# Preparing the seven-product pairs in three pieces and starting a head's attention every five ticks

## The chip, the cores and the metric

The kernel runs on one core of one Trainium2 chip. A core has five engines that work side by side, each through its own instructions in program order: TensorE (PE; its weight loads are shown as PEld), VectorE (DVE), ScalarE (ACT), GpSimd (POOL) and SyncE (SP), which here only starts transfers. The metric is the device time of one execution in microseconds (us); the median of several runs is given.

## The reference

One layer of a decoder: MoBA attention with 16 heads of 128, then a SwiGLU feed-forward block, each followed by a residual and a layer normalisation. There are 256 tokens of width 2048 and the inner width is 5632. With 256 tokens there is one MoBA block, so attention is plain causal attention with a bias by distance (T5 buckets).

```python
q, k, v = jnp.split(x @ w_qkv, 3, axis=-1)          # 256 x 2048 each, 16 heads
...
l_own = (jnp.einsum('bhqd,bhjd->bhqj', qc, k_own).astype(jnp.float32)
         + bias_h[:, t5_bucket(qpos[:, None] - kpos_own[None, :])].astype(jnp.float32))
p = masked_softmax(...)                              # causal
return ... + jnp.einsum('bhqj,bhjd->bhqd', p[..., n_sel:], v_own)
...
x = layer_norm(ALPHA * x + h, ln1_g[i], ln1_b[i])    # h = attention @ w_o
x = layer_norm(ALPHA * x + swiglu(x, ffn_w_gate[i], ffn_w_up[i], ffn_w_down[i]), ln2_g[i], ln2_b[i])
```

## The kernel before

**Sections, blocks and ticks.** Every large product is a *section*: `q0` to `q5` (the twelve 512-column chunks of `w_qkv`, two a section), `o0`, `o1` (`w_o`), `f0` to `f10` (a chunk of `w_gate` and one of `w_up` each) and `d` (`w_down`). A section goes through eight (`d`: 22) *pairs* of 128-row slices of its weights. The program is one list of *blocks*, PE's matmuls for one pair and one half of the rows or products; the index in that list is the *tick*. Ticks 18 to 33 are q1, 34 to 49 q2, 50 to 65 q3, 66 to 81 q4, 82 to 97 q5, 98 to 113 o0.

**Split numbers.** Each fp32 operand is taken as a high and a low part in `fp32r`: ACT copies it to the high part (L86), DVE subtracts (L87), and a product of two such operands is three matmuls (L278 to L280, or L342, L343 and L346).

**Seven products.** Sections q1 to q5 and f1 to f10 combine the halves of the rows so that fewer products are needed. In most pairs a half block is 12 matmuls. Pairs 1, 3 and 5 (`ST`) use a scheme with seven products: the first half block is 9 matmuls and the second 12. Such a pair is prepared by `split_quad`: two loads, four sums on DVE (`t13`, `t24`, L257 to L260), and the splits of `gq`, `uq` (raw) and of `aq`, `bq` (from the sums). A section of this kind keeps seven sums (`acc`) in seven of the eight PSUM banks; `sums_1`, `sums_2`, `sums_3` read them out four ticks before its last, one before and behind it. Banks are taken from the front of one queue (`bank`) and put back at its end (`give`), so a step that takes a bank waits until its last reader is done with it.

**Order.** At each tick the program writes first the work registered with `before`, then the pieces (load and split of a pair) whose start is due, then the block, then the work registered with `after`. A pair's pieces start 3 ticks ahead of its first block in the q sections (`AHEAD`), 6 or 5 in the f sections (`ST_AHEAD`), other numbers in places (`LEAD`, `EARLY`). Every engine executes its part of this order strictly. Tiles come from pools: `p4` (38 of 4 KB), `s2` (12 of 2 KB), `raw` (6, the loaded weights).

**Attention.** A group of four heads needs q, k from one section and v from another. A head goes through five steps: `at_t1` (four transposes of q and k into one bank, split into `qkh`, `qkl`), `at_s` (scores in a bank, bias and maximum on DVE, exponentials on ACT), `at_n` (reciprocal on DVE, scaling on ACT; no bank), `at_t2` (three transposes of the probabilities, split; split of v) and `at_o` (product with v, copied to the group's tile `o`). `att_steps` orders a group's steps, two heads at a time, so that a pair of heads takes eight ticks:

```python
one = [[(at_t1, a)], [(at_t1, b)], [(at_s, a)], [(at_s, b), (at_n, a)],
       [(at_n, b), (at_t2, a)], [(at_t2, b)], [(at_o, a)], [(at_o, b)]]
```

Group 0 runs in q2, group 1 in q3, group 2 in q5, group 3 in o0 (with fewer ticks); q4 has no attention. The results of groups 0 to 2 go to DRAM (`od`) and come back (`load_o`) before o0 needs them (`split_o`). `gate_t` transposes the hidden values of an f section through one bank each.

Of the kernel before, what the change touches and what calls it, by code (L numbers as in the profile page):

```python
# [11 lines left out]
F = mybir.dt.float32  # L12
# [4 lines left out]
P = 128  # L17
S = 256
# [19 lines left out]
AHEAD = 3  # L38
AHEAD_Q = 5
# [1 line left out]
SQK, SV = {0: 0, 1: 2, 2: 3, 3: 5}, {1: (0, 1), 4: (2, 3)}  # L41
KEEP = 2
ST = (1, 3, 5)
ST_AHEAD = {True: 6, False: 5}
WARM = 9
LEAD = {("f1", 0): 4, ("f1", 1): 3, ("d", 0): 6, ("d", 1): 4}
EARLY = {0: -1, 1: 0, 2: 1, 3: 2}


# [1 line left out]
def decoder_layer(ctx: ExitStack, tc: tile.TileContext, x, xt, rel_bias, w_qkv, w_o, g1, b1, gb1,  # L51
# [6 lines left out]
    dr = ctx.enter_context(tc.tile_pool(name="dr", bufs=1, space=bass.MemoryType.DRAM))  # L58
    ctx.enter_context(tc.manual_schedule())

    def p4(shape, dt, name):
        return sb.tile(shape, dt, tag="p4", bufs=P4, name=name)

    def s2(shape, dt, name):
        return sb.tile(shape, dt, tag="s2", bufs=S2, name=name)
# [6 lines left out]
    def bank(name):  # L72
        n = free.popleft()
        t = ps.tile([P, CW], F, tag=f"b{n}", bufs=1, name=name)
        held[id(t)] = (t, n)
        return t

    def give(*ts):
        for t in ts:
            free.append(held.pop(id(t))[1])  # L80

    def f32(t):
        return t.bitcast(F)

    def split(hi, lo, src):
        nc.scalar.activation(hi, src, AF.Copy)  # L86
        nc.vector.tensor_tensor(lo, src, f32(hi), op=OP.subtract)  # L87
# [11 lines left out]
    def load_x(p, ks):  # L99
        if p not in x_raw:  # L100
            x_raw[p] = s2([P, 2, S], F, f"xr{p}")
        nc.sync.dma_start(x_raw[p][:, ks, :], xt[p][:, ks, :])

    def split_x(p, ks):
        hi, lo = xT[p // 2]
        a = 2 * (p % 2)
        split(hi[:, a + ks.start:a + ks.stop, :], lo[:, a + ks.start:a + ks.stop, :], x_raw[p][:, ks, :])
# [15 lines left out]
    gbT = const.tile([P, 32], F, name="gbT")  # L123

    rows = dr.tile([H, RL], F, name="rows")
    od = dr.tile([3, P, 4 * S], F, name="od")
    bias_t = {}

    def load_small():
# [41 lines left out]
    def h_lhs(kt, m):  # L171
# [4 lines left out]
    Q = [Sec(f"q{n}", [(w_qkv, 4 * i + g) for i, g in pair], 8, x_lhs, xC if n else None)  # L176
         for n, pair in enumerate(QKV)]
    WO = [Sec(f"o{i}", [(w_o, 2 * i + c) for c in range(2)], 8, o_lhs) for i in range(2)]
    NF = FF // CW
    FU = [Sec(f"f{i}", [(w_gate, i), (w_up, i)], 8, x1_lhs, x1C if i else None) for i in range(NF)]  # L180
    DN = Sec("d", [(w_down, c) for c in range(4)], FF // (2 * P), h_lhs)
# [3 lines left out]
    def add(sec, pairs, m, chunks=None, ks=(0, 1)):  # L185
        blocks.append((sec, pairs, m, range(len(sec.chunks)) if chunks is None else chunks, ks))
        return len(blocks) - 1
# [13 lines left out]
    k = 8 - SKEW_WO  # L201
    alternate(WO[1], 0, k)
    wo_t = [[add(WO[1], list(range(k, 8)), m, [c]) for c in range(2)] for m in range(2)]
# [4 lines left out]
    k = DN.npair - SKEW_D  # L208
# [7 lines left out]
    first, last = {}, {}  # L216
# [4 lines left out]
    start = {k: t - AHEAD for k, t in first.items()}  # L221
    for p in range(1, 8):
        start["q0", p] = first["q0", p] - AHEAD_Q
    for p, t in EARLY.items():
        start["f0", p] = wo_t[0][0] + t
    for s in [*Q[1:], *FU[1:]]:
        for p in range(s.npair):
            start[s.name, p] = first[s.name, p] - (AHEAD if s in Q else ST_AHEAD[p in ST])
    for (n, p), a in LEAD.items():
        start[n, p] = first[n, p] - a  # L230
    order = sorted(((start[s.name, p], first[s.name, p], s, p) for s in [*Q, *WO, *FU, DN] for p in range(s.npair) if s is not Q[0] or p),
                   key=lambda v: (v[1], v[3]))

    def load_piece(s, p, c):
        w, col = s.chunks[c]
        r = sb.tile([P, 2, CW], F, tag="raw", bufs=RAW, name=f"r_{s.name}_{p}_{c}")
        src = w[p, col]
        if s is not Q[0] or p:
            nc.sync.dma_start(r, src)
        s.raws[p, c] = r, src  # L240

    def split_piece(s, p, c):
        if (p, c) not in s.raws:
            load_piece(s, p, c)
        r, _ = s.raws.pop((p, c))
        hi = p4([P, 2, CW], R, f"wh_{s.name}_{p}_{c}")
        lo = p4([P, 2, CW], R, f"wl_{s.name}_{p}_{c}")
        split(hi, lo, r)
        s.pieces[p, c] = (hi, lo)

    def split_quad(s, p):
        for c in range(2):
            if (p, c) not in s.raws:
                load_piece(s, p, c)
        (g, _), (u, _) = (s.raws.pop((p, c)) for c in range(2))
        t13, t24 = p4([P, 2, CW], F, "t13"), p4([P, 2, CW], F, "t24")
        nc.vector.tensor_tensor(t13[:, 0, :], g[:, 0, :], u[:, 0, :], op=OP.add)  # L257
        nc.vector.tensor_tensor(t13[:, 1, :], u[:, 0, :], u[:, 1, :], op=OP.add)  # L258
        nc.vector.tensor_tensor(t24[:, 0, :], t13[:, 0, :], u[:, 1, :], op=OP.add)
        nc.vector.tensor_tensor(t24[:, 1, :], t24[:, 0, :], g[:, 1, :], op=OP.add)  # L260
        g2 = [p4([P, 2, CW], R, "gq") for _ in range(2)]
        u2 = [s2([P, CW], R, "uq") for _ in range(2)]
        a2 = [p4([P, 2, CW], R, "aq") for _ in range(2)]
        b2 = [p4([P, 2, CW], R, "bq") for _ in range(2)]
        split(*g2, g)
        split(*u2, u[:, 1, :])
        split(*a2, t13)
        split(*b2, t24)
        at = lambda t, k: tuple(v[:, k, :] for v in t)
        s.pieces[p, 0] = s.pieces[p, 1] = {1: at(g2, 0), 2: at(g2, 1), 3: u2, 5: at(a2, 0), 7: at(a2, 1),  # L270
                                           6: at(b2, 0), 4: at(b2, 1)}

    def product(s, n, lhs, rhs, stop):
        start = n not in s.acc
# [107 lines left out]
    sums = {}  # L382
# [72 lines left out]
    def at_o(h):  # L455
        g, j = divmod(h, 4)
        hi, lo, vh, vl = att.pop(h)
        if j == 0:
            oT[g] = (p4([P, 4, S], R, f"oh{g}"), p4([P, 4, S], R, f"ol{g}")) if g == 3 else p4([P, 4, S], F, f"o{g}")
        b = bank("ov")  # L460
        n = 0
        for m, o, ks, w in ((0, 0, 0, 2 * P), (1, P, 2 * P, P)):
            for a, c in ((vh, hi), (vh, lo), (vl, hi)):
                nc.tensor.matmul(b[:, o:o + w], a[:, m, :], c[:, ks:ks + w], start=n == 0, stop=n == 5)
                n += 1
        if g == 3:
            oh, ol = oT[g]
            split(oh[:, j, :], ol[:, j, :], b[:, :S])
        else:
            nc.scalar.activation(oT[g][:, j, :], b[:, :S], AF.Copy)  # L470
            if j == 3:
                nc.scalar.dma_start(od[g], oT.pop(g))
        give(b)

# [9 lines left out]
    def att_steps(g):  # L484
        steps = []
        for a in (4 * g, 4 * g + 2):
            b = a + 1
            one = [[(at_t1, a)], [(at_t1, b)], [(at_s, a)], [(at_s, b), (at_n, a)],
                   [(at_n, b), (at_t2, a)], [(at_t2, b)], [(at_o, a)], [(at_o, b)]]
            if g == 3:  # L490
                one = [one[0] + one[1], one[2], one[3], one[4][:1], one[4][1:], one[5], one[6] + one[7]]
            steps += one
        return steps
# [156 lines left out]
    def before(t, f, *a):  # L650
        pre.setdefault(t, []).append((f, a))

    def after(t, f, *a):
        post.setdefault(t, []).append((f, a))
# [16 lines left out]
    for g in range(4):  # L671
        if g:
            at_sums(Q[SQK[g]], qk_sums, g)
        t0 = (first["q2", 0], first["q3", 0], first["q5", 0], first["o0", 0])[g]
        before(t0 - 3, load_bias, g)
        for n, step in enumerate(att_steps(g)):
            for f, h in step:
                after(t0 + n, f, h)
        if g < 3:
            after(first["o0", 2 * g] - 5, load_o, g)  # L680
            after(first["o0", 2 * g] - 3, split_o, g)
    after(last["o0", 0] - 6, reload_x)
    for m in range(2):
        for c in range(2):
# [19 lines left out]
    t = dn_t[0][0] - 32  # L704
# [5 lines left out]
    for i in range(NF):  # L710
        t = last[f"f{i}", 1]
# [10 lines left out]
    for i in range(NF):  # L722
        t = first["d", 2 * i]
# [14 lines left out]
    s = Q[0]  # L738
# [13 lines left out]
    n = 0  # L752
    for t, blk in enumerate(blocks):
        for f, a in pre.get(t, []):
            f(*a)
        while n < len(order) and order[n][0] <= t:
            _, _, ss, p = order[n]
            if ss is Q[0]:
                load_x(p, slice(0, 2))
                split_x(p, slice(0, 2))  # L760
            if ss.comb is not None and p in ST:
                split_quad(ss, p)
            else:
                for c in range(len(ss.chunks)):
                    split_piece(ss, p, c)
            n += 1
        block(*blk)
        for f, a in post.get(t, []):
            f(*a)
# [49 lines left out]
```

## Time and profile before

| what | value |
|---|---|
| median of 3 runs | 1145.39 us (1144.97 to 1145.89) |
| the profiled execution's own time | 1146.3 us |
| its span, first to last instruction | 1144.5 us |
| mean granted TensorE clock | 0.988 |
| busy: PE, PEld, DVE, ACT, POOL | 1105.3, 908.7, 867.8, 591.5, 10.3 us |
| read from HBM, written | 224.55 MB, 10.51 MB |

The profile is of one execution. Busy times of different engines overlap. PE's matmuls are pipelined and their ends are modelled, so that a busy PE is not PE at its peak. [...]

### The profile page before, as it was taken

Reading aid. Unit: us, or ns where it says so; the run is one execution under the profiler, and the core shown is the slowest. Engines: PE = TensorE matmul, PEld = TensorE weight load, DVE = VectorE, ACT = ScalarE, POOL = GpSimd, SP = SyncE. Lnnn points to the kernel's source line nnn. Section 1 sums busy time; section 2 is a strip of 40 time slices with the busy share of each in tenths; the row PEclk is TensorE's granted clock in tenths of the full one; section 3 lists DMA queues with packets and bytes.
Section 4 is the critical chain, followed back from the end, with each engine's and each line's share of the span. In section 5 each row is a group of like instructions: output and inputs, shape, how many; then the busy total and the mean of one; then the engine's idle time right before and its main releaser. Section 6 shows DMA issues by size and latency. Waiting matters only on the chain.

```text
span 1144.5 us, 13666 instructions
## 1 busy us (share of the span) xinstructions
PE 1105.3 (97%) x5004; PEld 908.7 (79%) x5004; DVE 867.8 (76%) x1124; ACT 591.5 (52%) x782; POOL 10.3 (1%) x16
## 2 busy tenths in 40 slices
PE   9998988998999999999999999999999999999995
PEld 6887777786778887788888888888888888888884
DVE  6897677788676867988988988988989546574446
ACT  6564555555556635655646646646647435353320
POOL 0000000000000000000000000000000000000001
PEclk9999998999999999999999999999999999999998
DMA  9574444473584825667566556556549595486611
GB/s 339 196 253 156 153 141 133 157 262 130 183 281 161 312 93 183 236 212 253 174 212 240 183 204 239 194 192 239 202 170 338 183 340 220 167 329 245 233 37 74
DMA packets 66611, 235.96 MB, mean 206 GB/s; under 512 B 7600, under 2 KB 8048, under 8 KB 66544
## 3 DMA queue, kind: packets, MB, share of 16 engines
q1 hardware_dynamic: 63632, 224.58, 56.2%
q10 hardware_dynamic: 2304, 8.39, 1.8%
q0 software_dynamic: 608, 2.12, 0.5%
q8 instruction: 39, 0.64, 0.2%
q14 instruction: 28, 0.23, 0.1%
HBM read 224.55 MB, written 10.51 MB: 205 GB/s over the span
## 4 chain that ended last, share of the span: by engine, by line
PE 82%; DVE 10%; ACT 4%; issue 2%; DMA 1%; SPq 0%; POOL 0%; ACTq 0%; DVEq 0%; POOLq 0%
PE acc_f L278 12%; PE acc_f L280 12%; PE acc_f L279 12%; PE acc_d L342 7%; PE acc_d L343 7%; PE acc_d L346 7%; PE acc_q L278 4%; PE acc_q L280 4%; PE acc_q L279 4%; PE acc_o L342 2%; PE acc_o L343 2%; PE acc_o L346 2%; PE acc_q L343 1%; PE acc_q L346 1%; PE acc_q L342 1%
## 5 line engine op out<-in xcount | busy, mean ns | idle before, releaser
L87 DVE TENSOR_TENSOR wl_d<-r_d,wh_d 128x1024 fp32r<-128x1024 f32 x88 | 104.4, 1222 | 71.5 <-ACT wh_d L86 50.8
L87 DVE TENSOR_TENSOR wl_f<-r_f,wh_f 128x1024 fp32r<-128x1024 f32 x116 | 135.2, 1219 | 16.1 <-ACT wh_f L86 15.9
L342 PE MATMUL acc_d<-wh_d,hh 128*128 128x512 f32 x352 | 137.0, 389 | 0.0
L343 PE MATMUL acc_d<-wl_d,hh 128*128 128x512 f32 x352 | 136.9, 389 | 0.0
L86 ACT ACTIVATE wh_d<-r_d 128x1024 fp32r<-128x1024 f32 x88 | 90.5, 1057 | 75.0 <-DMA r_d<-in_w_down 46.1
L86 ACT ACTIVATE wh_f<-r_f 128x1024 fp32r<-128x1024 f32 x116 | 115.7, 1049 | 9.1 <-DMA r_f<-in_w_up 4.0
L278 PE MATMUL acc_f<-wh_f,x1h 128*128 128x512 f32 x300 | 116.9, 390 | 0.0
L280 PE MATMUL acc_f<-wh_f,x1l 128*128 128x512 f32 x300 | 116.7, 389 | 0.0
L279 PE MATMUL acc_f<-wl_f,x1h 128*128 128x512 f32 x300 | 116.7, 389 | 0.0
L86 ACT ACTIVATE aq<-t 128x1024 fp32r<-128x1024 f32 x45 | 47.7, 1060 | 124.5 <-DVE t L258 114.6
L346 PE MATMUL acc_d<-wh_d,hl 128*128 128x512 f32 x352 | 99.9, 389 | 0.0
L87 DVE TENSOR_TENSOR wl_q<-r_q,wh_q 128x1024 fp32r<-128x1024 f32 x64 | 75.6, 1221 | 12.4 <-ACT wh_q L86 11.9
L346 PEld LDWEIGHTS acc_d<-wh_d,hl 128*128 128x128 f32 x352 | 66.1, 188 | 13.7
L342 PEld LDWEIGHTS acc_d<-wh_d,hh 128*128 128x128 f32 x352 | 66.1, 188 | 13.7
L343 PEld LDWEIGHTS acc_d<-wl_d,hh 128*128 128x128 f32 x352 | 66.1, 188 | 13.6
L86 ACT ACTIVATE wh_q<-r_q 128x1024 fp32r<-128x1024 f32 x64 | 64.1, 1048 | 3.3 <-DMA r_q<-in_w_qkv 2.9
L280 PEld LDWEIGHTS acc_f<-wh_f,x1l 128*128 128x128 f32 x300 | 56.3, 188 | 11.8
L278 PEld LDWEIGHTS acc_f<-wh_f,x1h 128*128 128x128 f32 x300 | 56.3, 188 | 11.6
L279 PEld LDWEIGHTS acc_f<-wl_f,x1h 128*128 128x128 f32 x300 | 56.3, 188 | 11.6
L278 PE MATMUL acc_q<-wh_q,xh 128*128 128x512 f32 x150 | 62.7, 418 | 0.0
L280 PE MATMUL acc_q<-wh_q,xl 128*128 128x512 f32 x150 | 60.2, 401 | 0.0
L279 PE MATMUL acc_q<-wl_q,xh 128*128 128x512 f32 x150 | 59.9, 399 | 0.0
(268 smaller groups left out, 2409.7 us busy)
## 6 DMA issues: line engine op xcount, KB each, us to landing
r_q<-in_w_qkv SPq DMA_DIRECT2D x94, 512.0 KB, 4.3
r_f<-in_w_gate SPq DMA_DIRECT2D x88, 512.0 KB, 3.8
r_f<-in_w_up SPq DMA_DIRECT2D x88, 512.0 KB, 4.9
r_d<-in_w_down SPq DMA_DIRECT2D x88, 512.0 KB, 6.1
r_o<-in_w_o SPq DMA_DIRECT2D x32, 512.0 KB, 4.4
hd<-hT ACTq DMA_DIRECT2D x9, 512.0 KB, 6.2
hT<-hd SPq DMA_DIRECT2D x9, 512.0 KB, 3.5
bias<-rows POOLq DMA_DIRECT2D x4, 512.0 KB, 5.6
```

Of the source, the lines that this page charges most:

```text
L86: nc.scalar.activation(hi, src, AF.Copy)
L87: nc.vector.tensor_tensor(lo, src, f32(hi), op=OP.subtract)
L278: nc.tensor.matmul(a, lh, rh, start=start, stop=False)
L279: nc.tensor.matmul(a, lh, rl, start=False, stop=False)
L280: nc.tensor.matmul(a, ll, rh, start=False, stop=stop)
L342: nc.tensor.matmul(a, lh, hi[:, k, :], start=kt == 0, stop=False)
L343: nc.tensor.matmul(a, lh, lo[:, k, :], start=False, stop=False)
L346: nc.tensor.matmul(s.acc[m, c], ll, hi[:, k, :], start=False, stop=kt == nk - 1)
```

## The change

`split_quad` becomes three functions, `quad_sums`, `quad_raw` and `quad_low`, that stand at three ticks one after another: in q sections 4, 3 and 2 ticks ahead of the pair's first block, in f sections 6, 5 and 4 (4, 3 and 2 for pair 1 of f1). The other pairs keep their starts. The list of pieces is sorted by start, not by first block. Attention of groups 0 to 2 no longer follows `att_steps`: a head's five steps stand three ticks apart, the heads five ticks apart, the groups twenty, from tick 34 on, so that heads of two groups follow each other through q4, and the last step of the twelfth head falls on tick 101. Group 3 keeps its place and steps. Group 2's result stays on the chip. `load_bias` stands two ticks ahead of a group, not three.

```diff
-ST_AHEAD = {True: 6, False: 5}
-LEAD = {("f1", 0): 4, ("f1", 1): 3, ("d", 0): 6, ("d", 1): 4}
+LEAD = {("d", 0): 6, ("d", 1): 4}
...
-    od = dr.tile([3, P, 4 * S], F, name="od")
+    od = dr.tile([2, P, 4 * S], F, name="od")
...
-    order = sorted(((start[s.name, p], first[s.name, p], s, p) for s in [*Q, *WO, *FU, DN] for p in range(s.npair) if s is not Q[0] or p),
-                   key=lambda v: (v[1], v[3]))
+    order = []
+    for s in [*Q, *WO, *FU, DN]:
+        for p in range(s.npair):
...
+            f = first[s.name, p]
+            if s.comb is None:
+                todo = [(start[s.name, p], "plain")]
+            elif p in ST:
+                a = 4 if s in Q or (s is FU[1] and p == 1) else 6
+                todo = [(f - a, "sums"), (f - a + 1, "raw"), (f - a + 2, "low")]
+            else:
+                todo = [(f - (3 if s in Q else 4 if s is FU[1] and not p else 5), "plain")]
+            order += [(t, f, p, what, s) for t, what in todo]
+    order.sort(key=lambda v: v[:3])
...
-    def split_quad(s, p):
+    quad = {}
+
+    def quad_sums(s, p):
         for c in range(2):
-            if (p, c) not in s.raws:
-                load_piece(s, p, c)
+            load_piece(s, p, c)
         (g, _), (u, _) = (s.raws.pop((p, c)) for c in range(2))
         t13, t24 = p4([P, 2, CW], F, "t13"), p4([P, 2, CW], F, "t24")
...
+        quad[s.name, p] = g, u, t13, t24
+
+    def quad_raw(s, p):
+        g, u, t13, t24 = quad[s.name, p]
         g2 = [p4([P, 2, CW], R, "gq") for _ in range(2)]
         u2 = [s2([P, CW], R, "uq") for _ in range(2)]
+        split(*g2, g)
+        split(*u2, u[:, 1, :])
+        s.pieces[p, 0] = {1: at_k(g2, 0), 2: at_k(g2, 1), 3: u2}
+
+    def quad_low(s, p):
+        _, _, t13, t24 = quad.pop((s.name, p))
         a2 = [p4([P, 2, CW], R, "aq") for _ in range(2)]
         b2 = [p4([P, 2, CW], R, "bq") for _ in range(2)]
-        split(*g2, g)
-        split(*u2, u[:, 1, :])
         split(*a2, t13)
         split(*b2, t24)
...
-            if j == 3:
+            if j == 3 and g < 2:
                 nc.scalar.dma_start(od[g], oT.pop(g))
...
-        t0 = (first["q2", 0], first["q3", 0], first["q5", 0], first["o0", 0])[g]
-        before(t0 - 3, load_bias, g)
-        for n, step in enumerate(att_steps(g)):
-            for f, h in step:
-                after(t0 + n, f, h)
-        if g < 3:
+        t0 = first["q2", 0] + 20 * g if g < 3 else first["o0", 0]
+        before(t0 - 2, load_bias, g)
+        if g == 3:
+            for n, step in enumerate(att_steps(g)):
+                for f, h in step:
+                    after(t0 + n, f, h)
+            continue
+        for j in range(4):
+            for f, n in ((at_t1, 0), (at_s, 3), (at_n, 6), (at_t2, 9), (at_o, 12)):
+                after(t0 + 5 * j + n, f, 4 * g + j)
+        if g < 2:
             after(first["o0", 2 * g] - 5, load_o, g)
-            after(first["o0", 2 * g] - 3, split_o, g)
+        after(max(first["o0", 2 * g] - 3, t0 + 28), split_o, g)
```

## Rows read from the trace of the kernel before

**Rows 1.** The page: engines' busy time; the chain that ended last, by engine.
```profile
PE 1105.3 (97%) x5004; PEld 908.7 (79%) x5004; DVE 867.8 (76%) x1124; ACT 591.5 (52%) x782; POOL 10.3 (1%) x16
...
PE 82%; DVE 10%; ACT 4%; issue 2%; DMA 1%; SPq 0%; POOL 0%; ACTq 0%; DVEq 0%; POOLq 0%
```

**Rows 2.** Stretches: their us, engines' busy us (instructions), granted clock, DMA share, GB/s.
```profile
94.20:318.40 224.20, 203.39 (x962) 167.53 (x962) 172.45 (x284) 123.08 (x212) 2.25 (x3) 0.95 0.50 166
...
480.00:1130.00 650.00, 650.00 (x2907) 538.13 (x2907) 493.82 (x550) 322.67 (x357) 0.99 (x1) 1.00 0.61 216
```

**Rows 3.** What PE waited for, whole span: us in total, times, longest.
```profile
PE t L447 <- ACT sc L441: 16.9, 6, 4.3
PE t L406 <- DVE k L379: 4.7, 2, 3.9
PE ht L631 <- ACT hT L632: 2.5, 1, 2.5
```

**Rows 4.** Timeline ahead of two waits of `at_t2`: start, us, engine, line, operation.
```profile
104.88 0.69 DVE L257 TENSOR_TENSOR t<-r_q,r_q 128x512 f32<-128x512 f32 x1
...
110.29 1.22 DVE L87 TENSOR_TENSOR bq<-t,bq 128x1024 fp32r<-128x1024 f32 x1
111.42 0.42 DVE L423 CUSTOM_DVE_ANT_0 sc<-lg,bias 128x256 f32<-128x256 f32 x1
...
113.19 0.49 ACT L440 ACTIVATE sc<-sc,rs 128x256 f32<-128x256 f32 x1
...
114.03 0.90 PE L447 MATMUL t<-ident,sc 128*128 128x128 f32 x3 [4.29 <-ACT sc L441]
...
143.20 0.55 PE L447 MATMUL t<-ident,sc 128*128 128x128 f32 x3 [1.50 <-ACT sc L441]
```

**Rows 5.** Timeline at tick 50, the transposes of k.
```profile
160.66 0.69 PE L406 MATMUL t<-ident,k 128*128 128x128 f32 x2 [3.92 <-DVE k L379]
```

**Rows 6.** Stretches about the long waits and one between them, columns as in rows 2.
```profile
112.50:119.30 6.80, 5.27 (x14) 4.30 (x15) 3.62 (x7) 4.85 (x12) 0.00 (x0) 0.50 0.06 17
160.30:163.70 3.40, 3.04 (x8) 2.47 (x9) 1.74 (x3) 2.32 (x3) 0.00 (x0) 0.50 0.50 205
177.30:184.10 6.80, 5.75 (x15) 4.57 (x16) 3.59 (x6) 4.48 (x10) 0.00 (x0) 0.50 0.15 33
279.80:283.10 3.30, 3.30 (x11) 2.62 (x10) 1.94 (x3) 3.04 (x6) 0.00 (x0) 0.50 0.00 0
119.40:160.20 40.80, 35.83 (x183) 29.53 (x181) 30.04 (x51) 21.26 (x39) 0.76 (x1) 1.00 0.48 159
```

**Rows 7.** Timeline at f0 to f1, the two `gate_t`.
```profile
477.77 0.58 ACT L632 ACTIVATE hT<-ht 128x512 f32<-128x512 f32 x1
...
478.40 0.66 PE L631 MATMUL ht<-ident,hn 128*128 128x128 f32 x4 [2.51 <-ACT hT L632]
```

**Rows 8.** Stretches without attention: of q4's length, and of f sections, columns as before.
```profile
215.00:256.50 41.50, 41.50 (x187) 34.44 (x186) 35.94 (x43) 23.21 (x27) 0.75 (x1) 1.00 0.75 253
...
530.00:800.00 270.00, 270.00 (x1215) 223.52 (x1214) 232.41 (x272) 146.97 (x170) 0.00 (x0) 1.00 0.62 213
```

**Rows 9.** Timeline of ACT and DVE behind `at_s`, `at_t2`, and `at_n`.
```profile
200.91 0.51 ACT L431 ACTIVATE sc<-sc,nm 128x256 f32<-128x256 f32 x1 [2.99 <-DVE nm L429]
...
202.88 2.36 DVE L87 TENSOR_TENSOR wl_q<-r_q,wh_q 128x1024 fp32r<-128x1024 f32 x2 [2.01 <-ACT wh_q L86]
...
212.53 2.36 DVE L87 TENSOR_TENSOR wl_q<-r_q,wh_q 128x1024 fp32r<-128x1024 f32 x2 [0.37 <-ACT wh_q L86]
...
331.77 0.49 ACT L440 ACTIVATE sc<-sc,rs 128x256 f32<-128x256 f32 x1
...
333.54 2.36 DVE L87 TENSOR_TENSOR wl_o<-r_o,wh_o 128x1024 fp32r<-128x1024 f32 x2 [2.43 <-ACT wh_o L86]
```

**Rows 10.** What DVE and ACT waited for from 94 to 322 us.
```profile
DVE qkl L87 <- ACT qkh L86: 8.1, 5, 1.9
...
ACT gq L86 <- DMA r_q<-in_w_qkv: 0.8, 1, 0.8
```

More of the change, by code (lines that the diff above doesn't have):

```diff
@@ L225, in decoder_layer @@
         start["f0", p] = wo_t[0][0] + t
-    for s in [*Q[1:], *FU[1:]]:
-        for p in range(s.npair):
-            start[s.name, p] = first[s.name, p] - (AHEAD if s in Q else ST_AHEAD[p in ST])
+    for p in range(1, 8):
+        start["q0", p] = first["q0", p] - AHEAD_Q
     for (n, p), a in LEAD.items():
         start[n, p] = first[n, p] - a
-    order = sorted(((start[s.name, p], first[s.name, p], s, p) for s in [*Q, *WO, *FU, DN] for p in range(s.npair) if s is not Q[0] or p),
-                   key=lambda v: (v[1], v[3]))
+    for p, t in EARLY.items():
+        start["f0", p] = wo_t[0][0] + t
+    order = []
+    for s in [*Q, *WO, *FU, DN]:
+        for p in range(s.npair):
+            if s is Q[0] and not p:
+                continue
[9 more added lines that the diff above has]
+    order.sort(key=lambda v: v[:3])
     def load_piece(s, p, c):
@@ L260, in split_quad, with at_k, plain @@
         nc.vector.tensor_tensor(t24[:, 1, :], t24[:, 0, :], g[:, 1, :], op=OP.add)
+        quad[s.name, p] = g, u, t13, t24
+    def at_k(t, k):
+        return tuple(v[:, k, :] for v in t)
+    def quad_raw(s, p):
+        g, u, t13, t24 = quad[s.name, p]
         g2 = [p4([P, 2, CW], R, "gq") for _ in range(2)]
         u2 = [s2([P, CW], R, "uq") for _ in range(2)]
+        split(*g2, g)
[3 more added lines that the diff above has]
+        _, _, t13, t24 = quad.pop((s.name, p))
         a2 = [p4([P, 2, CW], R, "aq") for _ in range(2)]
         b2 = [p4([P, 2, CW], R, "bq") for _ in range(2)]
-        split(*g2, g)
-        split(*u2, u[:, 1, :])
         split(*a2, t13)
         split(*b2, t24)
-        at = lambda t, k: tuple(v[:, k, :] for v in t)
-        s.pieces[p, 0] = s.pieces[p, 1] = {1: at(g2, 0), 2: at(g2, 1), 3: u2, 5: at(a2, 0), 7: at(a2, 1),
-                                           6: at(b2, 0), 4: at(b2, 1)}
+        s.pieces[p, 0].update({5: at_k(a2, 0), 7: at_k(a2, 1), 6: at_k(b2, 0), 4: at_k(b2, 1)})
+    def plain(s, p):
+        if s is Q[0]:
+            load_x(p, slice(0, 2))
+            split_x(p, slice(0, 2))
+        for c in range(len(s.chunks)):
+            split_piece(s, p, c)
     def product(s, n, lhs, rhs, stop):
@@ L673, in decoder_layer @@
             at_sums(Q[SQK[g]], qk_sums, g)
-        t0 = (first["q2", 0], first["q3", 0], first["q5", 0], first["o0", 0])[g]
-        before(t0 - 3, load_bias, g)
-        for n, step in enumerate(att_steps(g)):
-            for f, h in step:
-                after(t0 + n, f, h)
-        if g < 3:
+        t0 = first["q2", 0] + 20 * g if g < 3 else first["o0", 0]
[4 more added lines that the diff above has]
+                    after(t0 + n, f, h)
+            continue
+        for j in range(4):
+            for f, n in ((at_t1, 0), (at_s, 3), (at_n, 6), (at_t2, 9), (at_o, 12)):
+                after(t0 + 5 * j + n, f, 4 * g + j)
+        if g < 2:
             after(first["o0", 2 * g] - 5, load_o, g)
-            after(first["o0", 2 * g] - 3, split_o, g)
+        after(max(first["o0", 2 * g] - 3, t0 + 28), split_o, g)
     after(last["o0", 0] - 6, reload_x)
@@ L756, in decoder_layer @@
         while n < len(order) and order[n][0] <= t:
[L757 to L765, printed above, removed]
+            _, _, p, what, ss = order[n]
+            {"plain": plain, "sums": quad_sums, "raw": quad_raw, "low": quad_low}[what](ss, p)
             n += 1
```

## The prediction

> **What bounds the kernel now.** I read the page's engine table first, then the chain that ended last, then TensorE's busy time in stretches, then what TensorE waited for, and then the timeline around the longest waits. The table shows PE busy for 1105.3 us of 1144.5, and the chain runs 82% through PE and 10% through DVE [rows 1]. So PE sets the time, and only its idle stretches and its clock can be won back. The stretches say where those lie. From 480 to 1130 us PE has no idle microsecond [rows 2]; the feed-forward part has nothing to give. The 224.2 us from 94.2 to 318.4 are ticks 34 to 97, sections q2 to q5, where attention is interleaved with the products: PE is idle there for 20.8 us and its mean granted clock is 0.95 [rows 2].
>
> The list of PE's waits names three [rows 3]. The transposes of the probabilities (`at_t2`, L447) wait six times, 16.9 us in all, for ScalarE's normalisation (`at_n`). The transposes of q and k (`at_t1`, L406) wait twice, 4.7 us, for the last sum of k. The transpose of the first hidden block (`gate_t`, L631) waits once, 2.5 us. No wait of PE is for a DMA.
>
> The timeline shows what is late ahead of the first of the six [rows 4]. A quad's eight DVE instructions run in one piece from 104.88 to 111.42 us. The scores of head 1 lie ready in their bank, but their reduction stands behind the quad and begins at 111.42; the exponentials and the normalisation follow, and PE, which wants the probabilities of head 0 one tick after `at_n`, goes on only at 114.03 after 4.29 us. In tick 50 it is the same queue: the last sum of k runs behind a quad and lets PE go at 160.66 after 3.92 us [rows 5]. [...] The wait of 1.50 us at 143.20 lies in a stretch at 1.00 [rows 4, 6].
>
> **The change, part by part.** *Three pieces instead of one.* No instruction is added or removed: the two loads and four sums go to tick f-4 of a Q section, two splits to f-3, two to f-2 (f is the pair's first product), where all stood at f-3. Per tick DVE then has about 2.5 us of sums, 1.7 us (a split of 1.13 and one of half its size, 0.6) or 2.3 us (two of 1.13), not 6.5 us at once [rows 4]. Nothing comes too late by itself: the low pieces are for the second half block, at f+1. The loads' SP queue is governed by the six `raw` tiles, which the raw splits still release at f-3; ACT waited 0.8 us for weights in this stretch [rows 10]. I cost it at nothing; were that cover gone, a load would show up as an ACT wait. In the f sections the splits end one and two ticks later than before, but PE never waits there (270 us, no idle) and DVE is busy 232.4 of 270 us [rows 8]; nothing again.
>
> *Attention at five-tick steps.* A head now takes t1, s, n, t2, o at distances of three ticks, and a head starts every five ticks from tick 34 to 89. With n and t2 three ticks (some 8 us) apart, the six waits of L447 lose their cause: 16.9 us. Group 1 starts at tick 54, five ticks behind its sums, so the 3.92 us at tick 50 go; the other wait for k, 0.8 us, I leave, because group 3 keeps its place. With these the 8.7 us of clock go. The work itself stays: PE without these losses needs 224.2 - 20.8 - 8.7 = 194.7 us for the 64 ticks. Only the last two steps of head 11 move to ticks 98 and 101, behind which group 3's first transposes queue on PE; they wait for k there anyway.
>
> *f0 to f1.* The 2.5 us are a bank: the second `gate_t` needs the bank of the first, whose copy ran at 477.77, queued on ACT behind the two late splits of a quad [rows 7]. In the new order those splits (the "low" of pair 3) come two ticks after that copy's place, and pair 1's begin two ticks earlier. I take the 2.5 us as gone.
>
> *Group 2's store and reload* fall away, `load_bias` goes one tick nearer to its group on POOL's queue, but still five ticks ahead of `at_s`. Nobody waited for these: nothing.
>
> Losses removed: 16.9 + 3.9 + 2.5 + 8.7 = 32.0 us.
>
> **What comes in their place.** DVE was hidden half the time by PE's waiting. A section without attention costs DVE 35.94 us in the 41.5 us that PE needs [rows 8]. The stretch has 172.45 us of DVE work [rows 2], so a head costs DVE (172.45 - 4 x 35.94)/12 = 2.4 us; PE pays (194.7 - 4 x 41.5)/12 = 2.4 us for one too. In five ticks, one head, that is 13.6 us of DVE against 15.2 of PE: it fits. But DVE and ACT run in program order, and a split's low part waits for ACT's high part, which stands behind the step of the tick before. After the scores' reduction ACT does two exponentials and then the high split, and DVE stands for 2.0 us. After `at_n` ACT does the two scalings and the split: from 331.77 to 333.54, 1.8 us. After t2 it is 0.37 us [rows 9]. The loss arises only if the next tick begins with a split, not with sums or nothing. I went through the ticks: of 12 score steps 8 are followed by a split (ticks 38, 43, 53, 58, 63, 73, 83, 93), of 12 `at_n` also 8 (41, 51, 61, 66, 71, 81, 86, 91), of 12 t2 also 8. So DVE needs 172.5 + 8 x 2.0 + 8 x 1.8 + 8 x 0.37 = 205.9 us for 64 ticks of which PE could do in 194.7: PE must wait 11 us in total.
>
> It feels that through the banks: from a section's fourth to its twelfth tick seven of eight hold sums, so each step needs the bank of the step before it, read by DVE. Walking ticks 34 to 97 in order with these prices (a block of 12 matmuls 2.7 us by 187 in 41.5 us [rows 8], one of 9 2.0) gives waits of 3, 4, 5 and 5 us in q2 to q5, mostly 0.5 to 2.4 us each, where t2 needs the bank of the scores and t1 that of t2. The walk charged DVE 36.9 us a section, about 1 us too many in each, so 17 becomes 13, near the sum's 11. I take 13. Its ends: 0, if DVE's lag is absorbed everywhere; and, if every head pays 2.0 and the 2.43 us that one `at_n` shows with an exponential ahead of it, 0.37 and also the longest wait of `qkl`, 1.9 us [rows 9, 10], 13.6 + 6.7 = 20.3 against 15.2 us, 61 us for 12 heads.
>
> The profiled execution took 1146.3 us, 1.8 more than its span and 0.9 more than the median. 1146.3 - 32.0 + 13 = 1127.3; against the median 1126.4. I write 1126.5.
>
> **The rivals.** *PE-bound throughout.* DVE's waits fall into its own slack; everything is won: 1146.3 - 32.0 - 0.9 = 1113.4, up to 1119 with less than 6 us of new waits. For it speaks that DVE is busy only 172 of 194.7 us; against it the 2 us waits, which the order of the queues fixes.
>
> *Many short waits hold the clock down.* By the rows above only idle stretches of 3.7 us and more came with 0.50. If the new waits, close together, also draw it, with two drops a section at the mean price of before (8.7/4 = 2.2 us), 17 us more: 1144. One drop a section: 1135. [...]
>
> *DVE becomes the bound: slower.* One mechanism, the DVE-ACT-DVE turn after each step, in ticks 34 to 97. It decides when a head costs DVE and its turns 32/12 = 2.7 us more than PE's 15.2 us for five ticks; I count 13.6 + 2.0 + 1.8 + 0.4 = 17.8 when none of them is absorbed, 2.6 more, right at break-even; at the upper end, 20.3, it is 1146.3 - 32 + 61 - 0.9 = 1174. For it: quiet q4 loses its slack too, where DVE stood free today. Against it: a third of the turns is followed by sums or by nothing.
>
> *It does nothing:* the waits move from n-t2 to the banks in the same size, 28 to 36 us of new waits: about 1145.
>
> **How the numbers follow.** Chances: partial gain, 6 to 22 us of new waits, 0.57 (1119 to 1136, likeliest 1126.5); PE-bound 0.20 (1113 to 1119); clock 0.13 (1136 to 1144); nothing 0.04; slower 0.06. Whether a run differs can be told from about 0.2% on, 2.3 us. Faster by more: 0.57 + 0.20 + 0.13 = 0.90; within: 0.04; slower: 0.06. For 8 in 10 the range reaches from 1114 to 1140: half of the clock's cases, nothing and slower stay outside, together some 0.17.
>
> **What would show it.** In the changed profile: no L447 wait for `at_n`'s scaling; L406, L447 or L464 waiting 0.5 to 2.5 us for DVE's `ptl`, `qkl` or the scores' reduction, from the fourth tick of a section on; DVE busy about 83% of 208 us between the first product of q2 and of o0, against 77% of 224.2; granted clock 1.00 there; no 2.5 us ahead of L631. I am wrong if that stretch takes under 200 or over 218 us, if 0.50 still appears in it, if quads' pieces make PE wait (matmuls of `acc_q` waiting for a split), or if the f sections show idle time.

## The result and the profile after

The changed kernel takes 1128.82 us in the median (1128.10 to 1129.13, 4 runs), the kernel before 1145.64 (1144.97 to 1147.88, 4 runs): a ratio of 0.9849, 95% interval 0.9832 to 0.9866. The forecast was 1126.5 us, with a range from 1114 to 1140. The profiled execution took 1129.13 us, its span is 1127.0.

The engine table and the chain by engine, for [rows 1]:

```profile
PE 1099.1 (98%) x5004; PEld 904.6 (80%) x5004; DVE 866.9 (77%) x1124; ACT 589.3 (52%) x782; POOL 10.3 (1%) x16
...
PE 80%; DVE 11%; ACT 4%; issue 2%; DMA 1%; SPq 0%; POOL 0%; ACTq 0%; DVEq 0%; POOLq 0%
```

The instructions on the engines are the same in number; what PE lost to idle time and to a lower clock changed. Stretches of the changed kernel: ticks 34 to 97, the two places in them with a lower clock, and the f sections, with the columns of [rows 2, 6, 8]:

```profile
93.40:303.80 210.40, 198.07 (x952) 162.42 (x951) 168.75 (x279) 119.24 (x208) 2.25 (x3) 0.98 0.53 178
127.80:131.30 3.50, 3.50 (x11) 2.78 (x10) 2.25 (x3) 2.49 (x3) 0.00 (x0) 0.51 0.56 213
264.40:267.80 3.40, 3.40 (x10) 2.63 (x9) 3.37 (x6) 0.15 (x1) 0.00 (x0) 0.50 0.65 217
530.00:800.00 270.00, 270.00 (x1219) 223.48 (x1218) 234.30 (x277) 148.67 (x174) 0.00 (x0) 1.00 0.59 207
```

The 64 ticks take 210.4 us where they took 224.2. PE is idle for 210.4 - 198.07 = 12.3 us instead of 20.8, and half of the 6.9 us at about 0.50, 3.45 us, is put down as lost to the clock instead of 8.7. The half is an estimate: at 0.50 the products of 512 columns start 0.43 us apart (264.95, 265.37, 265.80 us), at 1.00 0.23 us (160.65, 160.88, 161.11). Without both, 194.6 us are left, against the 194.7 that the prediction took from the trace of before. What PE waited for, whole span, for [rows 3]:

```profile
PE t L436 <- DVE ptl L86: 6.5, 5, 2.4
PE t L477 <- DVE mx L455: 3.0, 4, 1.8
PE acc_q L308 <- DVE ptl L86: 2.8, 1, 2.8
```

None of the three waits of [rows 3] is left. The transposes of the probabilities (now L477) no longer wait for ACT's scaling but for their bank, until DVE has read the scores from it (`mx`); those of q and k (L436) wait for the bank whose reader is `ptl`; once a product of a section takes a bank that `ptl` still holds. The timeline of ticks 52 to 54 shows how this comes about (DVE, ACT and PE, in order of time):

```profile
157.80 0.69 DVE L274 TENSOR_TENSOR t<-t,r_q 128x512 f32<-128x512 f32 x1
158.41 0.42 DVE L453 CUSTOM_DVE_ANT_0 sc<-lg,bias 128x256 f32<-128x256 f32 x1
...
159.08 0.17 DVE L459 TENSOR_SCALAR nm<-mx 128x2 f32<-128x2 f32 x1
159.10 0.55 PE L477 MATMUL t<-ident,sc 128*128 128x128 f32 x3 [1.80 <-DVE mx L455]
159.28 0.51 ACT L461 ACTIVATE sc<-sc,nm 128x256 f32<-128x256 f32 x1 [4.50 <-DVE nm L459]
...
160.18 1.04 ACT L85 ACTIVATE gq<-r_q 128x1024 fp32r<-128x1024 f32 x1
161.25 1.23 DVE L86 TENSOR_TENSOR gq<-r_q,gq 128x1024 fp32r<-128x1024 f32 x1 [2.00 <-ACT gq L85]
...
163.00 0.55 DVE L86 TENSOR_TENSOR ptl<-t,pth 128x384 fp32r<-128x384 f32 x1
163.60 0.44 PE L436 MATMUL t<-ident,q 128*128 128x128 f32 x2 [1.18 <-DVE ptl L86]
```

DVE reaches the scores late, behind a pair's sums, and PE waits 1.80 us for the bank. Then DVE stands for 2.00 us, because ACT does the exponentials first and the high part of `gq` after them; `ptl` comes later by that, and PE waits another 1.18 us. What DVE waited for in the 64 ticks, the splits of weights first:

```profile
DVE wl_q L86 <- ACT wh_q L85: 20.6, 13, 2.1
DVE gq L86 <- ACT gq L85: 7.8, 4, 2.0
DVE aq L86 <- ACT aq L85: 5.9, 3, 2.0
...
DVE wl_o L86 <- ACT wh_o L85: 1.1, 1, 1.1
```

These waits for high parts make 35.4 us in 21 places; the prediction had counted 8 x 2.0 + 8 x 1.8 + 8 x 0.37 = 33.4. In the timeline of ACT, 16 of the 21 are the two kinds of turn that it counted one by one: eight behind the exponentials, of 2.0 us each, and eight behind the scaling, seven of 1.9 us and one of 2.1, together 31.3 us. The other five, 4.0 us, stand behind other work of ACT. With its three further waits for ACT DVE stood for 39.3 us, and was busy for 168.75 of the 210.4: it had hardly any slack left. At f0 to f1 the two `gate_t` of [rows 7] run without a wait:

```profile
452.39 0.60 PE L661 MATMUL ht<-ident,hn 128*128 128x128 f32 x4
...
460.34 0.60 PE L661 MATMUL ht<-ident,hn 128*128 128x128 f32 x4
```

They stand 8.0 us apart, where they stood 10.8 us apart. The copy between them is ACT's `hT`. Here are the low splits ahead of it before (first line) and after:

```profile
475.42 1.06 ACT L86 ACTIVATE aq<-t 128x1024 fp32r<-128x1024 f32 x1 [3.18 <-DVE t L258]
...
452.59 1.06 ACT L85 ACTIVATE aq<-t 128x1024 fp32r<-128x1024 f32 x1
453.54 1.06 ACT L85 ACTIVATE bq<-t 128x1024 fp32r<-128x1024 f32 x1
454.49 0.59 ACT L662 ACTIVATE hT<-ht 128x512 f32<-128x512 f32 x1
```

The copy still stands behind two low splits, now those of pair 1, but their sums were made two ticks earlier, so ACT no longer stands 3.18 us for them.

### The profile page after: what moved, and what is told of

Read it like the earlier page. It is cut to its first block, busy times and chain, and to the rows that moved or that the text cites. A ratio compares the mean times of both kernels' runs of the same rounds, so it can differ in the third digit from the quotient of the medians.

```text
span 1127.0 us, 13641 instructions
## 1 busy us (share of the span) xinstructions
PE 1099.1 (98%) x5004; PEld 904.6 (80%) x5004; DVE 866.9 (77%) x1124; ACT 589.3 (52%) x782; POOL 10.3 (1%) x16
## 4 chain that ended last, share of the span: by engine, by line
PE 80%; DVE 11%; ACT 4%; issue 2%; DMA 1%; SPq 0%; POOL 0%; ACTq 0%; DVEq 0%; POOLq 0%
PE acc_f L308 12%; PE acc_f L310 12%; PE acc_f L309 12%; PE acc_d L373 7%; PE acc_d L376 7%; PE acc_d L372 7%; PE acc_q L308 3%; PE acc_q L310 3%; PE acc_q L309 3%; PE acc_o L372 2%; PE acc_o L376 2%; PE acc_o L373 2%; DVE wl_q L86 2%; PE acc_q L373 1%; PE acc_q L376 1%
## 5 line engine op out<-in xcount | busy, mean ns | idle before, releaser
L86 DVE TENSOR_TENSOR aq<-t,aq 128x1024 fp32r<-128x1024 f32 x45 | 54.8, 1219 | 6.0 <-ACT aq L85 5.9
```

## Experiments

The theory: with pieces and steps spread out, DVE still needs more than PE's time in ticks 34 to 97, because of its turns with ACT, and PE feels it through the one free bank. Its rivals: the bank and DVE's load do it without the turns; one half of the change alone brings the gain; ACT's amount of work is what counts. Ratios below are to the kernel before on the same chip, with their 95% intervals; the changed kernel's is 0.9849.

**The three pieces alone.** The old attention ticks with the new pieces:

```diff
...
-        for j in range(4):
-            for f, n in ((at_t1, 0), (at_s, 3), (at_n, 6), (at_t2, 9), (at_o, 12)):
-                after(t0 + 5 * j + n, f, 4 * g + j)
...
+        for n, step in enumerate(att_steps(g)):
+            for f, h in step:
+                after(t0 + n, f, h)
...
```

Group 2's store and reload and the tick of `load_bias` go back with them.

> The changed kernel with attention back in its old ticks; only the three pieces remain. Theory (DVE is delayed by its turns with ACT and PE feels it through the one free bank): the 6.5 us blocks on DVE are gone, so the long waits of the probabilities' transposes fall from about 4 to 1 to 2 us and the clock stays at 1.00, but four heads in 16 ticks still cost DVE more than PE; 10 to 16 us of waits stay in q2, q3 and q5, none in q4; 1126 to 1134 us. Rival (only the two adjacent ticks of scaling and transposes matter): the six waits stay at about 17 us and the time stays above 1138.

1138.86 us, 0.9927 (0.9913 to 0.9942): slower than the theory's numbers. The time lies where the rival had put it, above 1138; its waits, which were to stay at about 17 us, do not. What its PE waited for:

```profile
PE t L477 <- ACT sc L471: 11.5, 6, 2.7
PE t L477 <- DVE ptl L86: 5.0, 3, 2.2
PE t L436 <- DVE k L409: 2.4, 2, 1.7
```

The waits for the scaling shrank from 16.9 to 11.5 us, the longest from 4.3 to 2.7, but the transposes of a pair's second head now meet a second wait, for the bank, and the clock fell three times for 3.4 us each (its mean in the profiled execution is 0.991), which I had excluded. About half of the change's gain is here.

**The spread alone.** The kernel before with the changed kernel's attention ticks, quads in one piece (the mirror image of the edit above).

> The kernel before with the new attention ticks; quads stay in one piece. Theory: each 6.5 us block now holds up a step that needs the last bank in the ticks behind it, so PE waits 2 to 4 us behind most quads at a section's fourth and eighth tick, the clock drops again, and the 2.5 us at the hidden block's transposes are back; 1138 to 1147 us. Rival (spreading alone brings the gain): no wait over 2 us in q2 to q5, 1126 to 1132.

1141.32 us, 0.9951 (0.9936 to 0.9966), as the theory had it:

```profile
PE t L406 <- DVE ptl L87: 8.9, 4, 3.9
PE ht L631 <- ACT hT L632: 2.5, 1, 2.5
PE ov L464 <- DVE qkl L87: 1.8, 2, 1.4
```

The scaling is no longer waited for, but a quad in one piece still holds up `ptl`, by up to 3.9 us, and the clock fell three times here too (mean 0.992). Neither half does it: 0.73% and 0.49% alone, 1.51% together. The two halves added make 1.22%, so most of the gain adds up.

**Taking the turns away.** The exponentials and the scaling of groups 0 to 2 get steps of their own, `at_e` and `at_r`, one tick later, so that on ACT they stand behind the next tick's high splits and mostly find DVE's result ready. No work is added or left out.

```diff
+        att[h] = [sc, sm]
+        ex[h] = nm
+        if h >= 12:
+            at_e(h)
...
+    def at_e(h):
...
+    def at_r(h):
...
-            for f, n in ((at_t1, 0), (at_s, 3), (at_n, 6), (at_t2, 9), (at_o, 12)):
+            for f, n in ((at_t1, 0), (at_s, 3), (at_e, 4), (at_n, 6), (at_r, 7), (at_t2, 9), (at_o, 12)):
...
```

> The changed kernel with the exponentials and the scaling of a head of groups 0 to 2 issued one tick later than the reduction and the reciprocal, so that on ACT they stand behind the next tick's high splits and DVE's low splits need not wait for them. All work and all other ticks stay. Theory (the turns are what makes DVE slower than PE): DVE loses the 2.0 us gaps behind the reduction and the 1.9 us gaps behind the reciprocal; PE's waits in ticks 34 to 97 fall from 12.3 us to under 3, no 0.50 clock there; 1112 to 1117 us. Rival (DVE's load and the one bank alone make the waits): waits stay 9 to 13 us, 1125 to 1130.

1112.84 us (1112.46 to 1112.97), 0.9701 (0.9684 to 0.9717). What PE waited for in attention, ticks 34 to 97 as a stretch, and DVE's timeline at the place shown above:

```profile
PE t L495 <- DVE mx L455: 0.5, 1, 0.5
PE t L436 <- DVE k L409: 0.2, 1, 0.2
```

```profile
93.60:287.00 193.40, 192.92 (x953) 160.94 (x952) 167.79 (x278) 118.79 (x208) 2.25 (x3) 1.00 0.58 193
```

```profile
151.56 0.69 DVE L274 TENSOR_TENSOR t<-t,r_q 128x512 f32<-128x512 f32 x1
152.17 0.41 DVE L453 CUSTOM_DVE_ANT_0 sc<-lg,bias 128x256 f32<-128x256 f32 x1
...
152.84 0.17 DVE L459 TENSOR_SCALAR nm<-mx 128x2 f32<-128x2 f32 x1
152.92 1.22 DVE L86 TENSOR_TENSOR gq<-r_q,gq 128x1024 fp32r<-128x1024 f32 x1
154.05 0.69 DVE L86 TENSOR_TENSOR uq<-r_q,uq 128x512 fp32r<-128x512 f32 x1
154.66 0.55 DVE L86 TENSOR_TENSOR ptl<-t,pth 128x384 fp32r<-128x384 f32 x1
```

The split of `gq` follows the reduction at once, `ptl` begins 2.49 us behind the reduction's start instead of 4.59, and PE's 12.3 us of waits are 0.5 us; the clock is 1.00 in the 64 ticks and 0.996 in the mean of the execution. What ACT waited for at the exponentials and the scaling, in the changed kernel (first two lines) and here, in the 64 ticks:

```profile
ACT sc L470 <- DVE rs L469: 39.2, 12, 5.5
ACT sc L461 <- DVE nm L459: 37.7, 12, 5.1
...
ACT sc L488 <- DVE rs L478: 2.4, 2, 2.2
ACT sc L471 <- DVE nm L459: 1.4, 1, 1.4
```

That is the turn's other half: ACT stood for DVE's result, 76.9 us, with the next high split behind, and now 3.8 us. The same banks, the same load of DVE and ACT: the rival of bank and load alone falls. Not all of DVE's waits went: for high parts of weights and sums it still stands 12.3 us in ten places, up to 2.7 us where a scaling comes right behind the copy of `o`, and PE hardly feels it. The 64 ticks are 17.0 us shorter; PE's waits and the clock account for 11.8 + 3.45 = 15.3 us of that, and where the rest lies was not looked into. This version beats both kernels, the changed one by 16 us.

**One kind of turn at a time.** The same edit for the exponentials only, and for the scaling only.

> The changed kernel with only the exponentials one tick later. Theory (turns add up against DVE's slack): the gaps behind the reduction, 8 of 2.0 us, go and those behind the reciprocal stay; DVE then needs about 190 of PE's 195 us in ticks 34 to 97, so one kind of turn fits into the slack; PE's waits fall from 12.3 to 1 to 5 us, 1113 to 1120 us. Rival (each turn costs PE its own share): half of the gain of both, about 1121.

> The changed kernel with only the scaling one tick later. Theory: the gaps behind the reciprocal, 8 of 1.9 us, go; those behind the reduction stay, and they stand right ahead of the steps that need the last bank, so somewhat more stays than with the exponentials moved: PE's waits 2 to 7 us, 1114 to 1122 us. Rival (each turn costs PE its own share): about 1121; rival (only the reduction's turn matters): 1127 to 1129.

1118.91 us, 0.9764 (0.9748 to 0.9779), and 1119.01 us, 0.9764 (0.9749 to 0.9778). PE's waits for banks in the first:

```profile
PE t L486 <- DVE mx L455: 3.1, 3, 1.9
...
PE acc_q L308 <- DVE ptl L86: 1.1, 1, 1.1
...
PE lg L449 <- ACT o L509: 0.7, 1, 0.7
```

and in the second:

```profile
PE t L436 <- DVE ptl L86: 4.2, 4, 1.5
...
PE acc_q L308 <- DVE ptl L86: 1.2, 1, 1.2
```

Either kind leaves 5 to 6 us of the 12.3. With the reduction's turn gone, `ptl` is nearly on time and what is left is mostly the scores' bank; with the reciprocal's gone, it is the other way round. Both times lie in the theory's ranges, but so near to half of the gain that they don't tell slack filled up from a share per turn.

**More work in a turn, and outside it.** A second scaling by 1.0, which changes no value, right behind the first, or a tick later:

```diff
+    def at_more(h):
+        sc, _ = att[h]
+        nc.scalar.activation(sc[:, :2 * P], sc[:, :2 * P], AF.Identity, scale=1.0)
+        nc.scalar.activation(sc[:, 2 * P:], sc[:, 2 * P:], AF.Identity, scale=1.0)
...
-            for f, n in ((at_t1, 0), (at_s, 3), (at_n, 6), (at_t2, 9), (at_o, 12)):
+            for f, n in ((at_t1, 0), (at_s, 3), (at_n, 6), (at_more, 6), (at_t2, 9), (at_o, 12)):
...
```

The second of the two runs has `(at_more, 7)` instead.

> The changed kernel with each scaling of groups 0 to 2 followed at once by a second one by 1.0, which changes no value and adds 0.7 us of ACT to the turn behind the reciprocal. Theory: DVE loses 0.7 us at each of 8 heads and PE, which waits for DVE already, waits some 4 to 6 us more; 1132 to 1136 us. Rival (ACT at half load has room, the turn is not what holds PE up): within 1 us of the changed kernel.

> The same second scaling, but issued one tick later, behind that tick's splits. Theory: as much more work on ACT, but outside the turn: at most 2 us slower than the changed kernel, 1128 to 1131. Rival (ACT's added work itself delays the splits and banks): as slow as the one before, 1132 to 1136.

1131.51 us, 0.9876 (0.9859 to 0.9892), and 1131.66 us, 0.9874 (0.9859 to 0.9889). The first cost less than forecast, the second a little more, and they agree: this pair doesn't tell a turn from ACT's work. "Outside the turn" was badly thought: work that stands behind one tick's splits on ACT stands ahead of the next tick's. So the question went to the kernel without turns: the same second scaling there, behind the scaling at its new tick.

> The kernel with exponentials and scaling one tick later, and a second scaling by 1.0 right behind the first (0.7 us more ACT work a head, no value changes). Theory (it is the order of the queues, not ACT's amount of work, that holds DVE and then PE up): with the turns gone the same added work costs nothing, within 1.5 us of that kernel without it, 1112 to 1115 us, PE's waits under 2 us. Rival (ACT's work itself is what costs, as the two runs with a second scaling suggest): 2.5 us more or over, from 1115.3 on.

1114.01 us, 0.9724 (0.9706 to 0.9742), by the medians 1.2 us more than without it, at the limit of what can be told, and inside the theory's numbers. Its PE waits:

```profile
PE t L500 <- DVE mx L455: 1.0, 1, 1.0
...
PE t L436 <- DVE k L409: 0.7, 1, 0.7
```

By the medians 0.7 us of ACT work a head cost 2.7 and 2.8 us in the changed kernel and 1.2 in the one with the later steps. By the ratios it is 0.27% and 0.25% against 0.23%, with overlapping intervals. So the added work costs little in either, and that it costs less with the turns gone is not shown; what is shown is that order alone, with no work changed, is worth 16 us.

**Are the three pieces needed without the turns?** Quads in one piece, attention at the new ticks, exponentials and scaling a tick later.

> Attention at the new ticks with exponentials and scaling one tick later, but the quads in one piece at their old ticks. Theory (the three pieces are still needed, because a 6.5 us block holds up a step that needs the last bank): waits of 1 to 3 us behind quads stay, 5 to 12 us in all, and the 2.5 us at the hidden block; 1119 to 1130 us. Rival (with the turns gone DVE has slack enough for blocks): 1113 to 1117, only the 2.5 us more than with both.

1130.84 us, 0.9863 (0.9847 to 0.9879): 18 us more than with three pieces. PE's longest waits:

```profile
PE t L406 <- DVE ptl L87: 5.5, 3, 3.2
PE t L465 <- DVE mx L425: 2.9, 3, 1.5
PE ht L649 <- ACT hT L650: 2.5, 1, 2.5
```

In ticks 34 to 97 PE was idle for about 10 us, inside the forecast; the time is 1 us above it, with three drops of the clock (mean 0.991), one of them at f0 to f1. Whether the spread is needed too once the turns are gone (three pieces, the old attention ticks, later exponentials and scaling) was not run.

**The f sections.** The changed kernel with the quads of f1 to f10 in one piece at their old ticks:

```diff
-                a = 4 if s in Q or (s is FU[1] and p == 1) else 6
-                todo = [(f - a, "sums"), (f - a + 1, "raw"), (f - a + 2, "low")]
+                a = 4 if s in Q else 3 if s is FU[1] and p == 1 else 6
+                k = 1 if s in Q else 0
+                todo = [(f - a, "sums"), (f - a + k, "raw"), (f - a + 2 * k, "low")]
```

> The changed kernel with the quads of the f sections in one piece at their old ticks. Theory: only the wait of 2.5 us ahead of the second transposes of the first hidden block comes back, all else in the f sections stays without idle time; 1131 to 1132 us. Rival (the three pieces matter throughout the f sections, or not at all there): no change, 1129, or idle time in several f sections, over 1134.

1131.23 us, 0.9862 (0.9847 to 0.9876), and the wait is back at its place, to the hundredth:

```profile
461.95 0.66 PE L662 MATMUL ht<-ident,hn 128*128 128x128 f32 x4 [2.51 <-ACT hT L663]
```

No other wait of PE came up in the f sections, so the three pieces are worth 2.5 us there, at this one place.

## Why the prediction was right

**The losses removed.** The 16.9 us at the probabilities' transposes, the 3.9 us for k and the 2.5 us at f0 to f1 are gone as forecast. The mechanisms of the first and the last stand on experiments: with either half undone, the first come back as waits behind ACT or behind a quad, and undoing the f part brings back the 2.51 us. The 0.8 us for k, which I had left standing, went too. Two readings behind the last were wrong: pair 1's pieces begin one tick earlier than before, not two, and the copy still stands behind two late splits, as its lines above show; what went is ACT's wait for sums made in the same tick. The loads, put at nothing, cost nothing: ACT waits for no load in the 64 ticks.

**What came in their place.** I had put down 13 us of new waits, from a sum (11) and a walk through the ticks (17, corrected to 13); 12.3 us came, in the places named: t2 for the scores' bank, t1 for that of t2. By sections the walk had 3, 4, 5 and 5 us; the trace has about 3 in each. That the turns make them is shown by the run that takes the turns away. Their number came as counted, eight of each kind, and nearly so their size: 2.0 us, and 1.9 where it had 1.8.

**The clock was mis-sized.** The step "with these the 8.7 us of clock go" was too large: 5.2 us went. No run shows the 8.7 us as such: they are half of the 17.4 us that PE was busy in the four stretches at 0.50 [rows 6]. What the traces show is products of 512 columns starting every 0.43 us at 0.50 and every 0.23 us at 1.00, before as after, which makes about 0.47 instead of the half, 8.1 us before and 3.2 after. From four waits of 3.7 to 4.3 us with a drop and one of 1.50 without I had read that only the long ones draw it. Behind the waits of 2.36 and 2.81 us the granted clock fell to 0.50 for 3.4 us each. That 0.50 still appears in this stretch was one of the signs by which the prediction said it would be wrong, and on this step it was. The rival that many short waits hold the clock down was right in kind, since both drops stand behind waits for banks, and far off in size: two drops, not eight, 3.45 us, not 17.

**The sum again.** 1146.3 - (16.9 + 3.9 + 2.5 + 5.2 + 0.8) + 12.3 = 1129.3 against 1129.13 profiled. Terms missed in opposite directions, 3.5 us of clock against 0.8 of k and 0.7 of waits; what is left, 2.0 us, is but for 0.2 the distance from 1127.3 to 1129.13. So a part of the closeness is errors that offset each other.

**The other rivals.** PE-bound throughout needed the turns to go; with both kinds of them gone the time was 1112.8, where that rival had put 1113.4. DVE as the bound, slower: its break-even, 32 us of new waits, was not approached. The wait that the prediction named as proof against itself, a product of `acc_q` waiting, came once, 2.81 us, though for a bank and not for a quad's split.

## What to carry to other kernels

Where engines execute in program order, count not only each engine's busy time per stage but the turns: A's result to B, B's next piece behind it, and back to A. Eight turns of 2 us of each kind were worth 16 us here, and they went without changing any work, by writing the middle engine's long operation behind the pieces that the first engine wants next. Splitting a long block and spreading the steps that share a buffer each gave a third to a half of this change's gain alone: without the split a block still held the shared bank, without the spread the transposes still came too soon behind the scaling. With the turns gone, leaving the blocks whole still cost 18 us.

## What the runs showed of the hardware that was not expected

The granted clock didn't follow the length of a wait alone. The first wait of 2.3 to 2.4 us in q2, for the bank of `ptl`, was followed by 0.50 in the changed kernel (2.36 us), with the spread alone (2.36) and with the second scaling a tick later (2.33), and not with the second scaling at once (2.35) or with the f sections in one piece (2.34). The 2.51 us at f0 to f1 were followed by 0.50 in the two runs that had quads in one piece in q and f alike and attention at the new ticks, but not in the kernel before, nor in the run with the f sections alone in one piece. With only the exponentials moved, a wait of 1.93 us was followed by a drop, while with the spread alone one of 2.14 us was not. What decides between these was not tried. A profile is of one execution, and the number of drops may differ between executions of one kernel: with the f sections in one piece the profiled one had a mean clock of 0.995 and took 1130.2 us, the other three 0.993 and 1131.1 to 1132.3. So the 3.45 us of clock are those of the profiled execution.
